# Where a seven-product sum is added to the residual, and which down panels of a gated MLP use seven products

## The chip, the cores and the metric

One core of a Trainium2 chip runs the whole program in one launch. The metric is the device time of an execution in microseconds (us), the median of several runs. Engines are called as in the profile: PE (TensorE, the matmuls), DVE (VectorE), ACT (ScalarE), POOL (GpSimd), SP (SyncE).

## The reference

Two layers of a decoder trunk over 256 tokens of width 2048, in fp32. Layer 0 mixes by gated linear attention, layer 1 by attention with forget gates; both also attend to 256 memory tokens. Behind each mixer stands a gated MLP of hidden width 5632, and this is where the change lies:

```python
def conv_ffn(h, w_up, conv_w, conv_b, w_down):
    u = causal_dwconv(h @ w_up, conv_w, conv_b)
    a, val = split_cols(u, [FFN_HIDDEN, FFN_HIDDEN])
    return (jax.nn.silu(a) * val) @ w_down

        h = rmsnorm(x, norm_ffn[i])
        x = x + conv_ffn(h, ffn_w_up[i], ffn_conv_w[i], ffn_conv_b[i], ffn_w_down[i])
    return rmsnorm(x, norm_final)
```

## The kernel before, in words

**Weights.** They come in units of 512 KB (two chunks of 128 rows by 512 columns and the like, a tile 128x1024) on SP's queue into a ring of slots `raw`. ACT rounds a unit to a high part (`whi`, L259, or L407 in a seven pair), DVE subtracts that for a low part (`wlo`, L260 or L408). The rings have five slots each and, in the MLP, one guest more, named `moremk` (high) and `moremv` (low) in layer 0 and `more` in layer 1. A product of two fp32 matrices is made of three passes of PE: high by high, low activations by high, high by low; each matmul is 128x128 by 128x512 into a bank of PSUM (`acc`, or the work banks `ps_o`, `ps_s`, `ps_t`).

**The residual.** `x[0]` to `x[3]` (x_64 to x_67 in the lists below) lie in SBUF, 512 columns each, two blocks b of 128 tokens. `add_to(f)` (L525) adds a bank or a tile to `x[f][:, b]` on DVE.

**The MLP.** The 44 hidden chunks of 128 are worked in three parts, PARTS = ((0, 16), (16, 28), (28, 44)). An up panel (`up_pair(j)`) makes four hidden chunks, whose results are turned, sent through memory and back (the transfers of L677 and L682, on Pool's queue), run through the convolution (taps, L1445 on ACT, L1452 on DVE) and gated into `m` (names `mix`, A, B). When a part's chunks are ready, its down panels add their products to x: `down_pair(l, p, f, ...)` is a wide panel for x[f] and x[f+1] at once, for f=0 and f=2 in the first two parts and for f=0 in the last. A counter `tick` at each step hands out the convolution's steps.

**Seven products.** `pair_steps` runs such a wide panel unit by unit, each unit one chunk of 128 rows by 1024 columns. For a pair of chunks (k, k+1) listed in `sums`, it uses Winograd's form of the 2x2 block product: seven products p1 to p7 and `x` in place of eight, 21 matmuls in place of 24. It needs sums of activations (made beforehand into `usum` or `dsum` tiles by `token_sums`) and of weights: the low part of w1 (512 columns) and w2, four differences of 512 columns (L464 to L467, in place in `raw`), and the low parts of w3 and w4 (`split_more`, L408). The matmul is at L437. When the last such pair of a panel is done, `early` takes the banks p1, p5, p6, p7 together and adds them to the four tiles of x; the banks of the other four products stay open for the rest of the panel, and `late` adds them to x at the panel's end by `add_to`. `at_step` says at which step which pair is taken, by default a pair at the step of its own number; the single units fill the other steps in order.

Before, part 0 has two pairs: f=0 takes pair 10 by seven products, f=2 pair 4 (FIRST_DOWN = (10,)), and each takes the other by eight. Before the up panels that follow, f=2 of part 0 lets three steps run, then frees the tile `dsum1` for the sums of an up panel (`input_sums(THIRD)`).

A scheduler orders the instructions of each engine, by priority and its own estimates; `issue_after` and `high_priority` steer it.

Of the kernel before, what the change touches and what calls it, by code (L numbers as in the profile page):

```python
# [16 lines left out]
AF = mybir.ActivationFunctionType  # L17
ALU = mybir.AluOpType
# [24 lines left out]
FIRST_DOWN = (10,)  # L43
# [83 lines left out]
def _layout():  # L127

    where, off = {}, 0
    for key, _, kcs, cols, per in _panels():  # L130
        n = sum(c[1] for c in cols)
        units = []
        for u in range(0, len(kcs), per):
            units.append((off, kcs[u : u + per], n))
            off += P * per * n
        where[key] = units
    return where, off
# [17 lines left out]
def _trunk(ctx: ExitStack, tc: tile.TileContext, xt, xtok, memt, wp, wgu, gns, gfin, cnv, par, msk, out):  # L155
    nc = tc.nc
    where, _ = _layout()
    V, S, TE = nc.vector, nc.scalar, nc.tensor
# [4 lines left out]
    x = [rear.tile([P, 2, 512], F32, name=f"x{f}") for f in range(4)]  # L163
# [13 lines left out]
    part = const.tile([P, P], F32, name="part")[:, :C_N]  # L177
# [345 lines left out]
    def add_to(f):  # L523

        return lambda b, a: V.tensor_tensor(x[f][:, b, :], x[f][:, b, :], a, ALU.add)  # L525
# [844 lines left out]
                    steps[f](u)  # L1370


    def down_pair(l, p, f, src, sums, flip, pool, temps, then=None):

        def early(bank):
            t0, t1 = temps()
            S.activation(t0, bank["p1"], AF.Copy)
            add_to(f)(0, t0)
            V.tensor_tensor(t0, bank["p6"], t0, ALU.add)
            V.tensor_tensor(t1, bank["p7"], t0, ALU.add)  # L1380
            add_to(f)(1, t1)
            add_to(f + 1)(1, t1)
            add_to(f + 1)(1, bank["p5"])
            V.tensor_tensor(t0, bank["p5"], t0, ALU.add)
            add_to(f + 1)(0, t0)

        def late(b, h, a):
            held_back = then is not None and h and not b and then.rooms is not None
            with tc.issue_after(then.turned[-1].ins) if held_back else nullcontext():
                add_to(f + h)(b, a)  # L1390
            if then is not None:
                then(f + h, b)

        return pair_steps(where["down", l, p, f], src, sums, flip, pool, early, late, {k: k for k in sums})

    def add_out(key, src, then=None, spare=None, last=None, first=0, hooks=None, late=1):

# [23 lines left out]
    def ffn(l, nx, h, m, more, ys, zs, landing, then, pool, temps, last=None, spare=None):  # L1421
        with tc.tile_pool(name=f"ffn{l}", bufs=1) as fp:
            def held(name, i):
                return pool.tile([P, 2, 4, P], F32R, name=name, tag=f"{name}{i}")
# [12 lines left out]
            count = [0, 0, 0]  # L1437
            sums = {}
# [34 lines left out]
            def input_sums(k):  # L1473

                r = temps(3).rearrange("p (s t) -> p s t", s=2)
                for s in range(2):
                    V.tensor_tensor(r[:, s, :], h[k + s][:, 0, :].bitcast(F32), h[k + s][:, 1, :].bitcast(F32), ALU.add)
                token_sums(r, up_sums[k])
# [28 lines left out]
            def tick(share):  # L1507

                clock[0] += 1
                credit[0] = min(credit[0], 0.0) + share  # L1510
                while returns and returns[0][0] <= clock[0] and not unread[returns[0][1]]:
                    _, slot, back, steps = returns.pop(0)
                    back()
                    unread[slot] = 12
                    waiting.extend(steps)
                while waiting and waiting[0][0] <= clock[0] and credit[0] > 0:
                    _, cost, step = waiting.pop(0)
                    credit[0] -= cost
                    step()
# [34 lines left out]
            def drive(steps, share=1.45):  # L1554
                for k in steps:
                    tick(share if k >= 0 else 0.0)

            def drive_up(j):
                drive(up_pair(j), 1.7 if j // 4 in MORE_IN else 1.45)
# [6 lines left out]
            for p, (lo, hi) in enumerate(PARTS[:-1]):  # L1566
                while done < hi + 4:
                    drive_up(done)
                    done += 4
                src = [m[c % RING] for c in range(lo, hi)]  # L1570
                for f in (0, 2):
                    count[2] += 1
                    steps = down_pair(l, p, f, src, {c - lo: t for c, t in sums.items() if (c in FIRST_DOWN) == (f == 0)}, count[2] % 2, pool,
                                      lambda: (temps(0), temps(1)))
                    if f and not p:
                        for _ in range(3):
                            next(steps)
                            tick(1.45)
                        up_sums[THIRD] = held("dsum", 1)
                        input_sums(THIRD)  # L1580
                    drive(steps)
                sums.clear()
            lo, hi = PARTS[-1]
# [2 lines left out]
                done += 4  # L1586
            p = len(PARTS) - 1
            src = [m[c % RING] for c in range(lo, hi)]
            wide = down_pair(l, p, 0, src, {c - lo: t for c, t in sums.items()}, 0, pool, lambda: (temps(0), temps(1)), then)

            def third(b, a):
                add_to(2)(b, a)
# [37 lines left out]
    def preparing(name, dst, pool, far, kept=None, tag="blk", queue=nc.sync):  # L1630

        n = StreamNorm()
        blocks, rooms, turned_blocks = {}, {}, []
        away, landed = [], []

        def land(z=None):  # L1640

            f, back = away.pop(0)
            if z is None:
                z = pool.tile([P, 4, 4, 2, 32], F32, name="turn", tag="turn", bufs=2) if kept is None else kept[f]
            with tc.issue_after((loads if queue is nc.sync else sent)[-1].ins):
                back(flat(z))
            landed.append((f, z))

        def take():

            f, z = landed.pop(0)
            with tc.issue_after(casts[-1].ins):
                for k in range(4):
                    split_turned(dst, 4 * f + k, z, name)

        def then(f, b):
            n.add(f, b)
            with tc.high_priority(offset=AHEAD):
                if b == 0:
                    blocks[f] = rooms[f]() if f in rooms else pool.tile([P, 4, 4, 2, 32], F32, name="blk", tag=tag, bufs=2)  # L1660
                y = blocks[f]
                turned_blocks.append(V.transpose(y[:, :, :, b, :],
                                                 x[f][:, b, :].rearrange("p (k c i) -> p c k i", c=4, i=32)))
                if b:
                    with tc.issue_after(sent[-1].ins) if queue is nc.gpsimd else nullcontext():
                        away.append((f, far_away(far, flat(y), T, queue)))

        n.rooms = then.rooms = rooms
        then.turned = turned_blocks
        n.land = then.land = land  # L1670
        n.take = then.take = take
        return n, then

    n = gla(nx)
    with tc.tile_pool(name="stash", bufs=1) as st:
        vt = st.tile([P, 2, FOX_H * HD], F32, name="fvt")
        turned3 = vt.rearrange("p b t -> p (b t)").rearrange("p (f q k b j) -> p f q k b j", f=3, q=4, k=4, b=2)
        turned3 = [turned3[:, f] for f in range(3)]

        with tc.tile_pool(name="turn1", bufs=1) as tp:  # L1680
            n2, then = preparing("kv", bufB, tp, dram, turned3, "raw2", nc.gpsimd)
            ys = [const.tile([P, 4, 4, 2, 32], F32, name="yu", tag=tag) for tag in ("mk0", "mv0")]
            fixed = [vt.rearrange("p b t -> p (b t)")[:, 2048 + 512 * i : 2560 + 512 * i] for i in range(2)]

            def temps(i):
                return fixed[i] if i < 2 else tp.tile([P, 512], F32, name="temp", tag=f"temp{i}")

            more = []
            for t, tag in ((mk, "mk1"), (mv, "mv1")):
                parked.append(dram.tile([P, 4 * T], F32, name="park" + tag, tag="park" + tag, bufs=1))  # L1690
                nc.gpsimd.dma_start(parked[-1], t[1].rearrange("p a b -> p (a b)"))
                more.append(const.tile([P, NUNIT], F32R, name="more" + tag, tag=tag))
            ffn(0, n, bufB, bufA, more, ys, turned3, ys, then, tp, temps)
        fox(n2, vt, turned3)
    with tc.tile_pool(name="turn2", bufs=1) as tp:
        n, then = preparing("ffn1", bufA, tp, dram)
# [7 lines left out]
    with tc.tile_pool(name="store", bufs=1) as op:  # L1704
# [16 lines left out]
        def then(f, b):  # L1721
            fin.add(f, b)
            if f == 0 and b == 0:
                S.activation(junk, fin.sums[:, 0, 0:1], AF.Sqrt)
            V.tensor_tensor(x[f][:, b, :], x[f][:, b, :], gf[f], ALU.mult)
# [110 lines left out]
```

## Time and profile before

| what | value |
|---|---|
| median of three runs | 2203.38 us (2202.36 to 2203.61) |
| the profiled execution: its own time | 2202.76 us |
| its span in the profile | 2200.8 us |
| PE busy | 2189.7 us (99%) |
| DVE busy | 1854.8 us (84%) |
| ACT busy | 1441.9 us (66%) |
| POOL busy | 137.2 us (6%) |
| moved by DMA | 515.40 MB, 234 GB/s mean |

The profile is of one execution. Times of instructions count from the start of the span. In rows of the timeline the columns are start, duration, engine, line and operation, tile written <- tiles read, shapes; an "x2" is two instructions run together, and brackets give idle time and who ended it. Instructions are pipelined, so one's duration (1.22 us) is more than the distance of two starts.

### The profile page before, as it was taken

How to read it: one execution, taken by the hardware profiler on the slowest of the kernel's cores; microseconds unless marked ns; L12 is line 12 of the kernel's file. 1: busy time of each engine (PE TensorE's matmuls, PEld its weight loads, DVE VectorE, ACT ScalarE, POOL GpSimd, SP SyncE). 2: the span in 40 equal slices, each digit the busy share in tenths (PEclk: the TensorE clock that was granted, in tenths of full speed). 3: DMA queues.
4: the chain of work that ended last, by engine and by line, in shares of the span. 5: the costliest groups of instructions: out<-in, count | busy, mean ns of one | idle time of the engine just before them, and what ended most of it. 6: DMA issues, size and time to landing. Idle time of an engine off the chain costs nothing.

```text
span 2200.8 us, 30087 instructions
## 1 busy us (share of the span) xinstructions
PE 2189.7 (99%) x10273; PEld 1843.4 (84%) x10273; DVE 1854.8 (84%) x2769; ACT 1441.9 (66%) x2292; POOL 137.2 (6%) x257
## 2 busy tenths in 40 slices
PE   9999999999999999999999999999999999999998
PEld 7888888888888888888888998888888888888886
DVE  7768986679998889899987669768999898988996
ACT  6655655557785668757865555455878567765884
POOL 0000000001110011001010000000110001101100
PEclk9999999999999999999999999999999999999999
DMA  9777566777777577667777766776777657766783
GB/s 365 254 223 225 185 216 218 258 234 259 244 258 243 173 237 257 233 210 241 249 245 238 225 204 226 243 243 235 248 270 245 216 187 262 239 209 231 238 274 107
DMA packets 166289, 515.40 MB, mean 234 GB/s; under 512 B 20780, under 2 KB 42552, under 8 KB 166136
## 3 DMA queue, kind: packets, MB, share of 16 engines
q1 hardware_dynamic: 149064, 460.99, 63.1%
q0 software_dynamic: 16496, 51.71, 7.4%
q8 instruction: 80, 1.31, 0.2%
q10 hardware_dynamic: 576, 0.79, 0.1%
q14 instruction: 73, 0.60, 0.1%
HBM read 469.62 MB, written 43.79 MB: 233 GB/s over the span
## 4 chain that ended last, share of the span: by engine, by line
PE 99%; DMA 0%; DVE 0%; ACT 0%; issue 0%; SPq 0%; DVEq 0%
PE acc L437 30%; PE acc L364 26%; PE ps_s L437 15%; PE ps_o L437 8%; PE ps_t L437 7%; PE acc L290 3%; PE acc L335 3%; PE ps_s L364 2%; PE acc L394 2%; PE acc L288 1%; PE ps_s L1062 0%; DMA raw<-wp 0%; PE ps_o L728 0%; PE ps_s L728 0%; PE ps_s L1335 0%; PE ps_s L1108 0%
## 5 line engine op out<-in xcount | busy, mean ns | idle before, releaser
L260 DVE TENSOR_TENSOR wlo<-raw,whi 128x1024 fp32r<-128x1024 f32 (+2 forms) x608 | 723.7, 1199 | 180.4 <-ACT whi L259 168.6
L259 ACT ACTIVATE whi<-raw 128x1024 fp32r<-128x1024 f32 (+2 forms) x608 | 630.1, 1043 | 368.5 <-PE acc L364 141.5
L364 PE MATMUL acc<-whi,B 128*128 128x512 f32 (+3 forms) x1248 | 290.8, 369 | 0.0
L364 PEld LDWEIGHTS acc<-whi,B 128*128 128x128 f32 x1248 | 226.8, 188 | 28.1
L407 ACT ACTIVATE whi<-raw 128x1024 fp32r<-128x1024 f32 (+1 forms) x166 | 156.4, 942 | 123.2 <-DVE raw L465 39.9
L408 DVE TENSOR_TENSOR wlo<-raw,whi 128x1024 fp32r<-128x1024 f32 (+1 forms) x166 | 178.1, 1076 | 15.6 <-ACT whi L407 9.8
L437 PE MATMUL acc<-whi,B 128*128 128x512 f32 x652 | 172.3, 389 | 0.0
L437 PE MATMUL acc<-whi,mix 128*128 128x512 f32 x636 | 164.9, 389 | 0.0
L364 PE MATMUL acc<-wlo,B 128*128 128x512 f32 (+3 forms) x624 | 159.1, 369 | 0.0
L437 PEld LDWEIGHTS acc<-whi,B 128*128 128x128 f32 x652 | 122.4, 188 | 25.4
L437 PEld LDWEIGHTS acc<-whi,mix 128*128 128x128 f32 x636 | 119.4, 188 | 24.8
L1445 ACT ACTIVATE tap<-fvt,cw 128x256 f32<-128x256 f32 x264 | 123.6, 530 | 9.6 <-DMA fvt<-far 7.9
L1445 ACT ACTIVATE tap<-yzu,cw 128x256 f32<-128x256 f32 x264 | 123.5, 529 | 5.9 <-DMA yzu<-far 4.2
L364 PEld LDWEIGHTS acc<-wlo,B 128*128 128x128 f32 x624 | 114.2, 188 | 14.6
L1452 DVE TENSOR_TENSOR tap<-tap,tap 128x1024 f32<-128x1024 f32 x88 | 106.9, 1215 | 0.1
L437 PE MATMUL ps_s<-whi,mix 128*128 128x512 f32 x350 | 98.5, 389 | 0.0
L437 PE MATMUL acc<-wlo,B 128*128 128x512 f32 x326 | 96.9, 389 | 0.0
L437 PE MATMUL acc<-wlo,mix 128*128 128x512 f32 x318 | 91.7, 389 | 0.0
L437 PE MATMUL ps_s<-whi,B 128*128 128x512 f32 x276 | 78.3, 389 | 0.0
L437 PEld LDWEIGHTS ps_s<-whi,mix 128*128 128x128 f32 x350 | 65.7, 188 | 13.7
L437 PEld LDWEIGHTS acc<-wlo,B 128*128 128x128 f32 x326 | 61.2, 188 | 12.7
L364 PE MATMUL acc<-whi,mix 128*128 128x512 f32 x280 | 70.4, 390 | 0.0
(569 smaller groups left out, 4307.5 us busy)
## 6 DMA issues: line engine op xcount, KB each, us to landing
raw<-wp SPq DMA_DIRECT2D x741, 512.0 KB, 4.6
fvt<-far POOLq DMA_DIRECT2D x100, 128.0 KB, 4.7
raw<-wp SPq DMA_DIRECT2D x32, 384.0 KB, 3.5
far<-yu POOLq DMA_DIRECT2D x22, 512.0 KB, 3.4
far<-yzu POOLq DMA_DIRECT2D x22, 512.0 KB, 3.4
yzu<-far POOLq DMA_DIRECT2D x88, 128.0 KB, 4.5
raw<-wp SPq DMA_DIRECT2D x24, 388.0 KB, 3.8
x<-xtok SPq DMA_DIRECT2D x8, 512.0 KB, 7.3
```

Source lines behind the costliest of these rows:

```text
L259: casts.append(S.activation(hi[:, s], raw[:, s], AF.Copy))
L260: lows.append(V.tensor_tensor(lo[:, s], raw[:, s], hi[:, s].bitcast(F32), ALU.subtract))
L288: mm = TE.matmul(acc[p][c][:, :T], w[:, s], both[:, 0, :], start=False, stop=end and j == 3)
L290: mm = TE.matmul(acc[p][c], w[:, s], both, start=u == j == 0, stop=end and j == 3)
L335: mm = TE.matmul(acc[b][:, :n], src[kcs[j] - base][:, part, b * P : (b + 1) * P], w, start=u == 0 and low == part == j == 0, stop=u == end ...
L364: mm = TE.matmul(acc[b][:, :n], src[kc - base][:, part, b * P : (b + 1) * P], ready[low][:, j * room : j * room + n], start=i == low == pa ...
L394: mm = TE.matmul(acc[b][:, :n], src[kc - base][:, part, b * P : (b + 1) * P], w, start=i == low == part == j == 0, stop=i == end and low = ...
L407: casts.append(S.activation(hi[:, :n], src, AF.Copy))
L408: lows.append(V.tensor_tensor(lo[:, :n], src, hi[:, :n].bitcast(F32), ALU.subtract))
L437: r = TE.matmul(bank[name], x, w, start=name not in begun, stop=last)
L1445: S.activation(by_run(taps[i][:, s, c, i:]), zs[slot][:, :, 2 * c + s], AF.Copy if i else AF.Identity, bias=0.0 if i else w[3], scale=w[2 ...
L1452: V.tensor_tensor(taps[0], taps[0], taps[n][:, :, :, :T], ALU.add)
```

## The change

Two edits. First, `early`: before, DVE added the four sums to x itself (one ACT copy, three additions among the banks, five `add_to`). Now ACT copies p1 to a tile, DVE makes the four sums in four tiles by four additions (L1378 to L1381 of the new kernel), and four transfers on Pool's queue (L1383), 256 KB each, from SBUF to SBUF, add them to x where it lies (`accum_op=ALU.add`). It happens four times in a layer. Second, in part 0 both wide panels take both pairs, 4 and 10, by seven products: f=0 takes pair 4 at step 4 and pair 10 at step 10 of its plan (written {5: 4, 10: 10}, the key being the step), f=2 takes pair 10 at step 5 and pair 4 at step 10. f=2 lets eight steps run before `dsum1` is taken over, with a `tick` share of 0.0 for the steps that `pair_steps` yields as -1.

```diff
@@ -1370,19 +1370,17 @@
                     steps[f](u)
 
 
-    def down_pair(l, p, f, src, sums, flip, pool, temps, then=None):
+    def down_pair(l, p, f, src, sums, flip, pool, temps, then=None, at_step=None):
 
         def early(bank):
-            t0, t1 = temps()
-            S.activation(t0, bank["p1"], AF.Copy)
-            add_to(f)(0, t0)
-            V.tensor_tensor(t0, bank["p6"], t0, ALU.add)
-            V.tensor_tensor(t1, bank["p7"], t0, ALU.add)
-            add_to(f)(1, t1)
-            add_to(f + 1)(1, t1)
-            add_to(f + 1)(1, bank["p5"])
-            V.tensor_tensor(t0, bank["p5"], t0, ALU.add)
-            add_to(f + 1)(0, t0)
+            t = [temps(i) for i in range(4)]
+            S.activation(t[0], bank["p1"], AF.Copy)
+            V.tensor_tensor(t[1], bank["p6"], t[0], ALU.add)
+            V.tensor_tensor(t[2], bank["p7"], t[1], ALU.add)
+            V.tensor_tensor(t[3], bank["p5"], t[2], ALU.add)
+            V.tensor_tensor(t[1], bank["p5"], t[1], ALU.add)
+            for (b, h), part in zip(((0, 0), (0, 1), (1, 0), (1, 1)), t):
+                nc.gpsimd.dma_start(x[f + h][:, b, :], part, accum_op=ALU.add)
 
         def late(b, h, a):
             held_back = then is not None and h and not b and then.rooms is not None
@@ -1391,7 +1389,7 @@
             if then is not None:
                 then(f + h, b)
 
-        return pair_steps(where["down", l, p, f], src, sums, flip, pool, early, late, {k: k for k in sums})
+        return pair_steps(where["down", l, p, f], src, sums, flip, pool, early, late, at_step or {k: k for k in sums})
 
     def add_out(key, src, then=None, spare=None, last=None, first=0, hooks=None, late=1):
 
@@ -1570,12 +1568,11 @@
                 src = [m[c % RING] for c in range(lo, hi)]
                 for f in (0, 2):
                     count[2] += 1
-                    steps = down_pair(l, p, f, src, {c - lo: t for c, t in sums.items() if (c in FIRST_DOWN) == (f == 0)}, count[2] % 2, pool,
-                                      lambda: (temps(0), temps(1)))
+                    steps = down_pair(l, p, f, src, {c - lo: t for c, t in sums.items() if not p or (c in FIRST_DOWN) == (f == 0)}, count[2] % 2, pool,
+                                      temps, at_step=None if p else {5: 10, 10: 4} if f else {5: 4, 10: 10})
                     if f and not p:
-                        for _ in range(3):
-                            next(steps)
-                            tick(1.45)
+                        for _ in range(8):
+                            tick(1.45 if next(steps) >= 0 else 0.0)
                         up_sums[THIRD] = held("dsum", 1)
                         input_sums(THIRD)
                     drive(steps)
@@ -1586,7 +1583,7 @@
                 done += 4
             p = len(PARTS) - 1
             src = [m[c % RING] for c in range(lo, hi)]
-            wide = down_pair(l, p, 0, src, {c - lo: t for c, t in sums.items()}, 0, pool, lambda: (temps(0), temps(1)), then)
+            wide = down_pair(l, p, 0, src, {c - lo: t for c, t in sums.items()}, 0, pool, temps, then)
 
             def third(b, a):
                 add_to(2)(b, a)
```

DVE's order, at the end of panel f=2 of part 0 in layer 0. Before (fvt is one of the temporaries, tap_4117 a tile of the convolution, x_66 and x_67 the halves of this panel's residual):

```order
L525 TENSOR_TENSOR x_67<-x_67,fvt 128x512
L408 TENSOR_TENSOR wlo<-raw,whi 128x512
L1452 TENSOR_TENSOR tap_4117<-tap_4117,tap_4118 128x1024
L464 TENSOR_TENSOR raw<-raw 128x512
L408 TENSOR_TENSOR moremv_4106<-raw,moremk_4103 128x1024
L1452 TENSOR_TENSOR tap_4117<-tap_4117,tap_4119 128x1024
L465 TENSOR_TENSOR raw<-raw 128x512
L466 TENSOR_TENSOR raw<-raw 128x512
L467 TENSOR_TENSOR raw<-raw 128x512
L525 TENSOR_TENSOR x_66<-x_66,acc 128x512
L408 TENSOR_TENSOR wlo<-raw,whi 128x1024
L525 TENSOR_TENSOR x_66<-x_66,acc 128x512
```

The same place in the changed kernel, from the first addition of `early` on (its convolution additions are at L1450):

```order
L1378 TENSOR_TENSOR fvt<-ps_t,fvt 128x512
L408 TENSOR_TENSOR wlo<-raw,whi 128x512
L1379 TENSOR_TENSOR temp<-ps_s,fvt 128x512
L464 TENSOR_TENSOR raw<-raw 128x512
L408 TENSOR_TENSOR wlo<-raw,whi 128x1024
L1380 TENSOR_TENSOR temp<-ps_s,temp 128x512
L1381 TENSOR_TENSOR fvt<-ps_s,fvt 128x512
L465 TENSOR_TENSOR raw<-raw 128x512
L525 TENSOR_TENSOR x_66<-x_66,acc 128x512 x2
L260 TENSOR_TENSOR wlo<-raw,whi 128x1024
L466 TENSOR_TENSOR raw<-raw 128x512
L1450 TENSOR_TENSOR tap_4117<-tap_4117,tap_4118 128x1024
```

and on from there to the low part `moremv` of the up panel's first seven pair:

```order
L525 TENSOR_TENSOR x_67<-x_67,acc 128x512 x2
L467 TENSOR_TENSOR raw<-raw 128x512
L408 TENSOR_TENSOR wlo<-raw,whi 128x1024
L260 TENSOR_TENSOR wlo<-raw,whi 128x1024
L1450 TENSOR_TENSOR tap_4117<-tap_4117,tap_4119 128x1024
L408 TENSOR_TENSOR wlo<-raw_4114,whi 128x1024
L408 TENSOR_TENSOR wlo<-raw,whi 128x512
L408 TENSOR_TENSOR moremv_4106<-raw,moremk_4103 128x1024
```

Before, the last of `early` (the first row) stood ahead of the up panel's weights; now all of `early`, the differences L464 to L467 of the up panel's first pair and the panel's final adds to x_66 and x_67 stand between each other.

PE's order in the up panel that follows, around the end of its first seven pair (B_97 and on are chunks of its input, `dsum` the sums). Before:

```order
L437 MATMUL ps_s<-whi,B_101 128x512 x4
L437 MATMUL ps_t<-whi,B_101 128x512 x2
L437 MATMUL ps_o<-wlo,B_101 128x512
L437 MATMUL ps_s<-wlo,B_101 128x512 x2
L437 MATMUL ps_t<-wlo,B_101 128x512
L437 MATMUL acc<-whi,B_103 128x512 x2
L437 MATMUL acc<-wlo,B_103 128x512
L437 MATMUL ps_o<-moremk_4103,B_104 128x512 x2
L437 MATMUL ps_o<-moremv_4106,B_104 128x512
L437 MATMUL ps_s<-moremk_4103,usum 128x512 x2
L437 MATMUL ps_s<-moremv_4106,usum 128x512
L437 MATMUL ps_o<-whi,B_102 128x512 x2
```

In the changed kernel:

```order
L437 MATMUL acc<-moremv_4106,dsum 128x512
L437 MATMUL ps_s<-moremv_4106,B_100 128x512
L437 MATMUL ps_s<-whi,B_98 128x512 x2
L437 MATMUL ps_s<-wlo,B_98 128x512
L437 MATMUL ps_s<-whi,B_101 128x512 x2
L437 MATMUL ps_s<-wlo,B_101 128x512
L437 MATMUL ps_o<-whi,B_102 128x512 x2
```

Before, all eight matmuls of a unit with the high part ran together (B_101, into three kinds of bank); now the two into the second `ps_s` bank are held back for units B_98 and B_101 and run behind the pair's last low part, shortly ahead of the next unit, B_102.

## The prediction

> **What bounds the kernel now.** First the page: the span, the share of each engine, and the chain that ended last.
>
> ```profile
> span 2200.8 us, 30087 instructions
> PE 2189.7 (99%) x10273; PEld 1843.4 (84%) x10273; DVE 1854.8 (84%) x2769; ACT 1441.9 (66%) x2292; POOL 137.2 (6%) x257
> PE 99%; DMA 0%; DVE 0%; ACT 0%; issue 0%; SPq 0%; DVEq 0%
> ```
>
> TensorE (PE) is busy 2189.7 of 2200.8 us and holds 99% of the chain. The view of its waits names all that it waited for:
>
> ```profile
> PE ps_o L191 <- DVE B L188: 1.5, 1, 1.5
> PE acc L335 <- DVE A L562: 0.3, 1, 0.3
> PE acc L364 <- DVE wlo L260: 0.2, 1, 0.2
> PE acc L394 <- DVE wlo L260: 0.2, 1, 0.2
> ```
>
> That is 2.2 us in all, and none of it stands in a panel that the change touches. The chain in order of time gives the price of one matmul, where 144 of them stand behind each other in 32.64 us:
>
> ```profile
> 881.45 32.64 PE acc L437 x144
> ```
>
> 32.64 / 144 = 0.2267 us. So a matmul that goes is worth 0.2267 us, and work taken from VectorE (DVE) alone is worth nothing, as long as DVE is in time. What the change can lose is therefore read from how late DVE comes where the change puts work. The table of stretches shows DVE over the panel f=2 of part 0 (712.65 to 755.49 us in layer 0) and around it:
>
> ```profile
> 670.00:712.60 42.60, 42.60 (x189) 35.27 (x189) 38.45 (x53) 22.18 (x28) 5.48 (x10) 1.00 0.74 246
> 712.60:755.00 42.40, 42.40 (x188) 35.11 (x188) 36.83 (x44) 28.95 (x43) 0.00 (x0) 1.00 0.48 163
> 755.00:797.00 42.00, 42.00 (x187) 34.75 (x187) 38.57 (x46) 25.26 (x31) 0.00 (x0) 1.00 0.67 237
> ```
>
> Its third column of times is DVE: 38.45 of 42.60, 36.83 of 42.40, 38.57 of 42.00 us. PE has no gap, but DVE has little to spare (4, 5.5 and 3.5 us of some 42). This is the place to look at.
>
> **The matmuls.** A chunk pair by seven products takes 21 matmuls instead of 24. In part 0 f=0 now takes pair 4 as well and f=2 pair 10 as well: two pairs more in each of two layers, 4 × 3 = 12 matmuls fewer, and all lie on the path: 12 × 0.2267 = **-2.72 us**. This is also the most that can be won, but for the 2.2 us of waits elsewhere that the change does not touch.
>
> **DVE's work.** Its durations, from the timeline of DVE, by the distance from one start to the next:
>
> ```profile
> 732.44 2.35 DVE L260 TENSOR_TENSOR wlo<-raw,whi 128x1024 fp32r<-128x1024 f32 x2
> 734.71 1.22 DVE L260 TENSOR_TENSOR moremv<-raw,moremk 128x1024 fp32r<-128x1024 f32 x1
> 735.85 1.22 DVE L1452 TENSOR_TENSOR tap<-tap,tap 128x1024 f32<-128x1024 f32 x1
> 736.98 1.28 DVE L525 TENSOR_TENSOR x<-x,fvt 128x512 f32<-128x512 f32 x2
> 738.18 2.35 DVE L260 TENSOR_TENSOR wlo<-raw,whi 128x1024 fp32r<-128x1024 f32 x2
> ...
> 744.52 0.75 DVE L556 TENSOR_TENSOR mix<-tap,mix 128x256 fp32r<-128x256 f32 x2
> 745.20 0.68 DVE L525 TENSOR_TENSOR x<-x,fvt 128x512 f32<-128x512 f32 x1
> ```
>
> Two 1024-wide low parts take 734.71 - 732.44 = 2.27, one 1.135; two 512-wide additions take 738.18 - 736.98 = 1.20, one 0.60 (0.605 over longer runs). A seven pair costs DVE one low part of 512, three of 1024 and four differences of 512 instead of two low parts of 1024: 0.605 + 3 × 1.135 + 4 × 0.605 - 2 × 1.135 = +4.16; two in a layer, +8.3. Each end of the seven products drops from eight additions to four, 4 × 0.605 = -2.42, four in a layer, -9.7. So DVE gains 1.4 us in a layer, but in part 0 it has 8.3 - 4.8 = 3.5 us more. Off the path, DVE's balance costs nothing; what counts is where the 3.5 us falls.
>
> **The end of panel f=2, part 0.** The panel has lost three matmuls of f=0 ahead of it, and starts where this row stood, at 711.97:
>
> ```profile
> 711.97 0.62 PE L437 MATMUL ps_t<-whi,A 128*128 128x512 f32 x2
> 712.65 1.52 PE L437 MATMUL acc<-whi,mix 128*128 128x512 f32 x6
> 727.38 0.39 PE L437 MATMUL ps_t<-wlo,dsum 128*128 128x512 f32 x1
> 755.49 0.61 PE L437 MATMUL ps_o<-whi,B 128*128 128x512 f32 x2
> ```
>
> Before, the last product p6 was whole at 727.38 + 0.39, 28 us ahead of the next up panel (755.49), and the additions to x were spread over that time. Now pair 4 is the last seven pair, and its p6 low matmul is number 165 of the panel: 711.97 + 164 × 0.2267 = 749.15, whole at 749.54. DVE's in-order queue holds L1378 there, which waits for it; with it 22 instructions stand in DVE's order up to the end of the low part `moremv`, 8 of 1024 and 14 of 512: 8 × 1.135 + 14 × 0.605 = 17.55, so that low part is ready at 767.09. PE asks for it in the first seven pair of the up panel, 80 matmuls behind that p6: 749.15 + 80 × 0.2267 = 767.29. **0.2 us to spare.** The 17.55 us hold no idle time, so each wait put into them beyond 0.2 us comes out at PE.
>
> The accumulating transfers put one there. The residual adds of L525 at the panel's end (x_66, then x_67) must wait for the transfers into the same bytes to land. The x_66 transfer from `temp` is issued when L1379 is done, 749.54 + 3 × 0.605 = 751.36; DVE reaches the second add to x_66 after eight instructions of 512 and one of 1024, 8 × 0.605 + 1.135 behind 749.54, at 755.52. Cover: 4.16 us. (For x_67: 4.69.) So with a landing time L a layer loses max(0, L - 4.16 - 0.20) us. No transfer in the trace adds to its target. The nearest rows, all issued by Pool:
>
> ```profile
> far<-yu POOLq DMA_DIRECT2D x22, 512.0 KB, 3.4
> fvt<-far POOLq DMA_DIRECT2D x100, 128.0 KB, 4.7
> L682 POOL DMA_DIRECT2D fvt<-far x100: 550/552/583, 506.7 to 1152.5; - x100
> DMA to landing us min/median/max: 2.7/4.6/9.3
> DMA to landing us min/median/max: 2.9/3.4/9.4
> out<-x SPq DMA_DIRECT2D x4, 256.0 KB, 3.4
> ```
>
> The two lines of landing are those of L682 (into SBUF) and of L677 (out of SBUF). So L lies between 2.7 and 9.4; I take 4.4, between the medians and nearer to the transfers that land in SBUF as these do: 0.04 us. At 2.7 it costs nothing, at 9.4 it costs 5.0 us a layer.
>
> By the Trainium skill ("DMA: Bandwidth & Descriptors", section "Anatomy of one DMA — SWDGE (gpsimd) path") such a transfer takes about 2.0 us and its bytes at 436 GB/s, an estimate of 2.6 us for 256 KB; that would leave this term at zero. The trace's 128 KB into SBUF, with 4.7 us, are slower than it says.
>
> Two smaller terms stand in the same up panel. In PE's new order the products of unit 1 wait for the fourth low part, so between the last reading of one high part (B_98) and the first use of the one that takes its slot (B_102) stand 4 matmuls, 0.91 us, and the split takes one ACT operation:
>
> ```profile
> L259 ACT ACTIVATE whi<-raw 128x1024 fp32r<-128x1024 f32 (+2 forms) x608 | 630.1, 1043 | 368.5 <-PE acc L364 141.5
> ```
>
> 1.04 - 0.91 and the hand-overs give some 0.2 us. And the second seven pair's `w3` low part ends 6 × 1.135 + 9 × 0.605 = 12.3, with two short splits (L556, 745.20 - 744.52 = 0.68 for two) 12.9 us, behind unit 5's low part, where PE asks for it 55 matmuls = 12.47 us behind it: 0.3 us with the hand-over. Bounds of both: nothing, if the slot comes free in other places first, and twice as much. The sum for the place is 0.5 us a layer, and layer 1 has the same order row for row: **+1.1 us**.
>
> **Elsewhere.** The ends of f=0 in part 0, of f=2 in part 1 and of the wide last panel have the same four transfers, but 7 us or more lie between them and the adds that wait, and DVE has 2.4 us less to do in the last two: nothing, as long as L stays below 7; above it they too would hold DVE. Pool issues 16 transfers more in a layer, 0.55 us each as in the row of L682; Pool is busy 137.2 us, and what stands behind them on its queue belongs to an up panel's return more than 20 us later: nothing. SP's weight loads keep their order; the added 8 MB of traffic from SBUF to SBUF is 2% of the page's bytes: nothing at 0.48 of DMA share.
>
> **Sum.** -2.72 + 1.1 = -1.6 us. Made against the profiled execution's 2202.76: 2201.1. The median of the three runs is 2203.38, 0.62 above it: **2201.7**.
>
> **The rivals.** *All of it is won.* DVE is a little quicker than my sum over the 22 instructions and L is under 4.3: 2203.38 - 2.72 = 2200.7. For it: PE shows no gap today at places where DVE is 92% busy; against: 0.2 us to spare is less than my rows agree to.
>
> *The transfers land late.* An adding transfer has to read its target as well as its source. If it then takes twice as long as the plain one of 256 KB (3.4), L = 6.8, and each layer loses 6.8 - 4.36 = 2.44: -2.72 + 4.88 + 1.0 = +3.2, 2206.6. It is even at L = 5.2 and slower by over 0.2% from L = 7.4; at the 9.3 that L682's slowest took, +8.2, 2211.6. For it: the longest rows; against: the medians, and DMA is busy 0.48 of this stretch. The Trainium skill ("Collectives: The Full Stack", section "The bandwidth ceiling: the fold count and why AG ≠ RS ≠ AR") says that a reducing step takes two source reads and runs at half the rate of a copy; by it the sum would be this rival's. No run here shows such a transfer yet.
>
> *No change at all*, that the extra products are eaten by DVE's 3.5 us: they would have to be lost whole at the panel's end, 1.75 us a layer at L near 5.2. It lies between the forecast and the second rival.
>
> **How the numbers follow.** Forecast (2201.7, stalls of 0.2 to 1 us a layer) 47%; all won (2200.7) 29%; late landings 20%, of which 12% end below +4.4 us and 8% above; something that gains more 2%, something else that costs more 2%. A measurement tells 0.2%, 4.4 us, from no change. Faster by more would need more than the 12 matmuls: 0.02; slower by more: 0.08 + 0.02 = 0.10; within: 0.88. The range goes from all won less the 0.6 us by which profile and median differ, 2200.1, to a landing of 6.3 us, -2.72 + 3.88 + 1.0 = +2.1, 2205.5. What lies above (late landings beyond that) and below is some 16%.
>
> **What would show it.** Right: PE 10261 instructions, busy some 2.7 us less; its waits a few tenths at the first up panel behind part 0 (near 766 to 775 us, and 1033 us later in layer 1), for `moremv` or `wlo` of L408 or `whi` of L259; the transfers of L1383 land in 4 to 5 us. Wrong: a wait of DVE's L525 for the transfers of more than a microsecond, then PE waits of the same size; PE waits at other panels; or a landing time under 3 us with the stall still there.

## The result and the profile after

The changed kernel takes **2206.20 us** (median of 15 runs, 2204.12 to 2211.42), the one before 2202.77 (median of 15, 2201.92 to 2203.61): a ratio of 1.0017, interval 1.0010 to 1.0024, some 3.4 us slower. The forecast was 2201.7, its range ended at 2205.5. Against the full saving of the 12 matmuls, 2202.77 - 2.72 = 2200.05, the changed kernel has lost 6.1 us. The profiled execution took 2211.42 us, the slowest of the 15: against the same full saving it has lost 11.4 us, so the stalls read below are larger than those of the median run.

The page of the changed kernel, with its span, the share of the engines and the row of 24 of its 32 new transfers (the other eight carry `x<-fvt`):

```profile
span 2209.6 us, 30107 instructions
PE 2191.3 (99%) x10261; PEld 1841.6 (83%) x10261; DVE 1852.0 (84%) x2761; ACT 1445.8 (65%) x2300; POOL 165.1 (7%) x289
x<-temp POOLq DMA_DIRECT2D x24, 256.0 KB, 6.4
```

PE has its 12 matmuls fewer (10273 to 10261) and is still busy 1.6 us longer. DVE fell by 2.8 us, which is the 1.4 us a layer of the prediction. Pool is busy 27.9 us more for the 32 transfers. The view of waits names what PE waits for:

```profile
PE ps_o L437 <- ACT whi L259: 2.6, 4, 1.9
PE acc L437 <- ACT whi L259: 1.6, 1, 1.6
PE ps_o L191 <- DVE B L188: 1.5, 1, 1.5
PE ps_s L1334 <- ACT p L738: 1.4, 1, 1.4
PE ps_o L437 <- DVE wlo L260: 0.7, 1, 0.7
PE ps_s L437 <- ACT whi L407: 0.7, 1, 0.7
PE acc L364 <- ACT whi L259: 0.3, 1, 0.3
```

All rows but L191's are new, and nearly all name a weight split of ACT or DVE. (L1334's lies in the attention of layer 1, which the change leaves alone; experiments without transfers show it too, with 0.5 to 1.0.) The places of the loss are read from the starts of the matmuls, which lie apart by more than their 0.2267 us. In layer 0 that is so at 769 us (0.5 us in all), at 822 to 830 (4.8) and at 870 to 873 (some 1.7). In layer 1, 1033 us later, it is so at the same three places: 1807 to 1810 (0.7), 1863 to 1865 (0.4) and 1908 (2.2). The first of the three is the place that the prediction spoke of; the others lie one and two up panels later.

The table of stretches covers the last panel of part 0 and the three up panels behind it, first in the changed kernel, then in the one before, whose row of 755 to 797 us the prediction has shown:

```profile
711.00:755.00 44.00, 44.00 (x195) 36.44 (x195) 36.17 (x49) 26.76 (x41) 3.23 (x4) 1.00 0.63 198
755.00:797.00 42.00, 41.77 (x184) 34.13 (x183) 39.92 (x47) 25.99 (x31) 0.24 (x1) 1.00 0.70 233
797.00:840.00 43.00, 40.60 (x170) 32.57 (x169) 34.08 (x40) 29.27 (x45) 5.49 (x10) 0.96 0.68 218
840.00:882.00 42.00, 41.00 (x179) 33.14 (x178) 38.52 (x51) 29.94 (x49) 5.48 (x10) 1.00 0.70 245
```

```profile
711.00:755.00 44.00, 44.00 (x196) 36.44 (x195) 38.42 (x47) 28.95 (x43) 0.00 (x0) 1.00 0.49 167
797.00:840.00 43.00, 43.00 (x191) 35.63 (x190) 37.55 (x47) 33.05 (x51) 5.54 (x10) 1.00 0.72 233
840.00:882.00 42.00, 42.00 (x187) 34.75 (x187) 41.72 (x52) 35.20 (x58) 5.50 (x10) 1.00 0.75 245
```

Read the third column of times, DVE. In the panel it is given one seven pair more and four additions less, 4.16 - 2.42 = some 1.7 us more by the prediction's prices, and yet it does 36.17 us instead of 38.42: it stands idle for 7.8 us, where it was for 5.6. The view of its waits says in this stretch for what:

```profile
DVE x L525 <- DMA x<-temp: 3.1, 2, 1.6
DVE wlo L260 <- ACT whi L259: 2.6, 3, 1.2
DVE fvt L1378 <- PE ps_t L437: 2.1, 1, 2.1
DVE x L525 <- DMA x<-fvt: 0.2, 1, 0.2
```

It waits 3.3 us for landings at f=0's end and 2.1 us for p6 of the late pair; the 2.6 us for ACT's splits were 2.5 before. What DVE didn't do there comes behind, in panels with little room: the last row of before has 41.72 of 42.00 us. And the third row of the changed kernel holds only 170 matmuls, at a mean granted clock of 0.96.

How lateness of DVE comes to PE can be followed in layer 0 over three engines. First come DVE's transposes that end the first up panel, from its timeline, before and after:

```profile
797.32 0.70 DVE L1492 STREAM_TRANSPOSE yu<-fvt 128x512 f32<-128x512 f32 x1
798.57 0.70 DVE L1492 STREAM_TRANSPOSE yu<-temp 128x512 f32<-128x512 f32 x1
```

```profile
798.78 0.70 DVE L1490 STREAM_TRANSPOSE yu<-fvt 128x512 f32<-128x512 f32 x1
801.77 0.70 DVE L1490 STREAM_TRANSPOSE yu<-temp 128x512 f32<-128x512 f32 x1
```

The second is 3.2 us later, though PE had come 1.4 us earlier to f=2's end and lost 0.5 since. Pool, which waits for it, sends the panel's first half away at 799.56 before and at 802.84 after. Its rows go on to the second half and to the loads that bring both back:

```profile
799.56 0.56 POOL L677 DMA_DIRECT2D far<-yu  x1 [109.12 <-DVE yu L1492]
802.54 0.56 POOL L677 DMA_DIRECT2D far<-yu  x1 [2.42 <-DMA far<-yu]
803.10 0.57 POOL L682 DMA_DIRECT2D fvt<-far  x1
```

```profile
802.84 0.56 POOL L677 DMA_DIRECT2D far<-yu  x1 [47.60 <-DVE yu L1490]
805.23 0.55 POOL L677 DMA_DIRECT2D far<-yu  x1 [1.83 <-DVE yu L1490]
808.37 4.38 POOL L682 DMA_DIRECT2D fvt<-far  x8 [2.59 <-DMA far<-yu]
```

The loads go out 5.3 us later. ACT stands at the first convolution tap until they have landed, and the weight splits that follow in its order start only behind it (before, then after):

```profile
812.78 2.91 ACT L1445 ACTIVATE tap<-fvt,cw 128x256 f32<-128x256 f32 x7 [2.64 <-DMA fvt<-far]
```

```profile
819.11 2.12 ACT L1443 ACTIVATE tap<-fvt,cw 128x256 f32<-128x256 f32 x5 [8.44 <-DMA fvt<-far]
```

ACT is idle for 8.44 us where it was for 2.64, and PE then waits for its splits. PE's timeline of the changed kernel shows this, and behind the waits a few slow matmuls:

```profile
821.13 0.39 PE L437 MATMUL acc<-moremv,usum 128*128 128x512 f32 x1
822.22 1.19 PE L437 MATMUL ps_s<-whi,usum 128*128 128x512 f32 x4 [0.69 <-ACT whi L407]
823.48 0.73 PE L437 MATMUL ps_s<-wlo,usum 128*128 128x512 f32 x2
825.84 2.93 PE L437 MATMUL acc<-whi,B 128*128 128x512 f32 x6 [1.63 <-ACT whi L259]
828.57 1.18 PE L437 MATMUL acc<-wlo,B 128*128 128x512 f32 x3
829.59 0.62 PE L437 MATMUL ps_t<-whi,usum 128*128 128x512 f32 x2
830.04 1.98 PE L437 MATMUL acc<-whi,B 128*128 128x512 f32 x8
```

From 825.84 to 828.57 six matmuls start, one per 0.455 us, twice the 0.2267. The granted clock of this stretch, the third number from the end, is 0.51:

```profile
825.80:828.60 2.80, 2.76 (x7) 2.18 (x8) 2.78 (x3) 2.80 (x4) 0.00 (x0) 0.51 0.24 64
```

From 821.13 to 830.04 there are 18 matmuls, 4.1 us of work in 8.9: 4.8 lost, of it some 1.7 to the slow matmuls. This is the one such place: in no other kernel's trace does a stretch of 20 us between 400 and 2180 us have a granted clock under 1.00.

In layer 1 the same chain costs less. ACT stands 5.54 us at the tap there, and PE loses only 0.4 us at 1863. The largest loss of layer 1, at 1908, has another wait ahead of it, that of a split for its weights:

```profile
1857.00 2.12 ACT L1443 ACTIVATE tap<-yzu,cw 128x256 f32<-128x256 f32 x5 [5.54 <-DMA yzu<-far]
1905.31 1.06 ACT L259 ACTIVATE whi<-raw 128x1024 fp32r<-128x1024 f32 x1 [1.51 <-DMA raw<-wp]
```

That load was issued at 1897.38, after 1.4 us of waiting for a low part of DVE (L408), and took 7.9 us to land, against a median of 4.5. Whether DVE's lateness is behind this wait too was not tried; the return is in any case not the only place where PE's time goes.

### The profile page after: what moved, and what is told of

The parts are those of the page before. It is cut to its first block, busy times and chain, and to the rows that moved or that the text cites. A ratio compares the mean times of both kernels' runs of the same rounds, so it can differ in the third digit from the quotient of the medians.

```text
span 2209.6 us, 30107 instructions
## 1 busy us (share of the span) xinstructions
PE 2191.3 (99%) x10261; PEld 1841.6 (83%) x10261; DVE 1852.0 (84%) x2761; ACT 1445.8 (65%) x2300; POOL 165.1 (7%) x289
## 4 chain that ended last, share of the span: by engine, by line
PE 93%; issue 4%; DMA 1%; ACT 1%; DVE 1%; POOL 0%; SPq 0%; DVEq 0%; ACTq 0%; POOLq 0%
PE acc L437 27%; PE acc L364 26%; PE ps_s L437 14%; PE ps_o L437 7%; PE ps_t L437 6%; PE acc L335 3%; PE acc L290 2%; PE ps_s L364 2%; PE acc L394 2%; PE acc L288 1%; PE ps_s L1062 0%; DMA fvt<-far 0%; ACT whi L259 0%; PE ps_o L728 0%; DMA far<-y 0%
## 5 line engine op out<-in xcount | busy, mean ns | idle before, releaser
L260 DVE TENSOR_TENSOR wlo<-raw,whi 128x1024 fp32r<-128x1024 f32 (+2 forms) x601 | 715.7, 1200 | 196.8 <-ACT whi L259 185.1
L259 ACT ACTIVATE whi<-raw 128x1024 fp32r<-128x1024 f32 (+2 forms) x601 | 622.8, 1043 | 370.7 <-PE acc L364 140.3
L364 PEld LDWEIGHTS acc<-whi,B 128*128 128x128 f32 x1248 | 226.8, 188 | 28.1
L407 ACT ACTIVATE whi<-raw 128x1024 fp32r<-128x1024 f32 (+1 forms) x180 | 169.5, 946 | 95.8 <-DVE raw L465 32.7
L408 DVE TENSOR_TENSOR wlo<-raw,whi 128x1024 fp32r<-128x1024 f32 (+1 forms) x180 | 194.0, 1082 | 22.3 <-ACT whi L407 17.4
L437 PE MATMUL acc<-whi,mix 128*128 128x512 f32 x644 | 168.7, 389 | 0.1
L437 PE MATMUL acc<-whi,B 128*128 128x512 f32 x606 | 163.1, 392 | 1.6 <-ACT whi L259 1.6
L437 PEld LDWEIGHTS acc<-whi,B 128*128 128x128 f32 x606 | 114.4, 189 | 25.9 <-ACT whi L259 2.1
L1450 DVE TENSOR_TENSOR tap<-tap,tap 128x1024 f32<-128x1024 f32 x88 | 106.9, 1215 | 1.7 <-ACT tap L1443 1.7
L437 PE MATMUL ps_s<-whi,mix 128*128 128x512 f32 x314 | 90.2, 389 | 0.0
L437 PE MATMUL ps_s<-whi,B 128*128 128x512 f32 x296 | 85.5, 389 | 0.0
L437 PEld LDWEIGHTS acc<-wlo,mix 128*128 128x128 f32 x322 | 60.4, 188 | 12.6
```

The costliest lines, as they stand in the source:

```text
L259: casts.append(S.activation(hi[:, s], raw[:, s], AF.Copy))
L260: lows.append(V.tensor_tensor(lo[:, s], raw[:, s], hi[:, s].bitcast(F32), ALU.subtract))
L364: mm = TE.matmul(acc[b][:, :n], src[kc - base][:, part, b * P : (b + 1) * P], ready[low][:, j * room : j * room + n], start=i == low == pa ...
L407: casts.append(S.activation(hi[:, :n], src, AF.Copy))
L408: lows.append(V.tensor_tensor(lo[:, :n], src, hi[:, :n].bitcast(F32), ALU.subtract))
L437: r = TE.matmul(bank[name], x, w, start=name not in begun, stop=last)
```

## The experiments

There were two theories at first. **A:** the extra seven pair in the last panel of part 0 makes DVE late, and PE is reached by the way just read. **B:** the accumulating transfers, which land in 6.4 us in the median and take Pool 0.87 us each, are the cost. The medians of the kernel before beside the runs were 2202.9 to 2203.0 us. "Lost" below is a kernel's distance from that (for the changed kernel from 2202.77), plus the 0.2267 us for each matmul that it saves.

| kernel | median, us | ratio to before (interval) | matmuls fewer | lost, us |
|---|---|---|---|---|
| changed kernel | 2206.20 | 1.0017 (1.0010 to 1.0024) | 12 | 6.1 |
| transfers only | 2203.14 | 1.0002 (0.9993 to 1.0011) | 0 | 0.2 |
| pairs only | 2211.59 | 1.0037 (1.0025 to 1.0050) | 12 | 11.3 |
| transfers, pair in f=0 only | 2201.70 | 0.9997 (0.9988 to 1.0006) | 6 | 0.1 |
| transfers, pair in f=2 only | 2209.72 | 1.0030 (1.0019 to 1.0042) | 6 | 8.1 |
| changed, taps later | 2203.57 | 1.0003 (0.9994 to 1.0012) | 12 | 3.3 |
| changed, pairs of f=2 at 3 and 7 | 2199.92 | 0.9987 (0.9978 to 0.9996) | 12 | -0.4 |
| pairs in f=0 of parts 0 and 1 | 2205.78 | 1.0012 (1.0003 to 1.0021) | 12 | 5.5 |
| before, DVE work added | 2205.69 | 1.0012 (1.0003 to 1.0021) | 0 | 2.7 |
| pairs at 3 and 7, no transfers | 2202.87 | 0.9999 (0.9990 to 1.0008) | 12 | 2.7 |
| changed, pairs of f=2 at 4 and 8 | 2199.60 | 0.9987 (0.9978 to 0.9996) | 12 | -0.6 |
| changed, pairs of f=2 at 2 and 5 | 2200.69 | 0.9990 (0.9982 to 0.9999) | 12 | 0.5 |

The intervals reach some 1.5 to 3 us to either side, so a "lost" below 2 us can't be told from none.

**The two halves alone.** First comes the changed kernel with the choice of pairs of before; `dsum1` is taken over after three steps again:

```diff
-  steps = down_pair(l, p, f, src, {c - lo: t for c, t in sums.items() if not p or (c in FIRST_DOWN) == (f == 0)}, count[2] % 2, pool,
-                    temps, at_step=None if p else {5: 10, 10: 4} if f else {5: 4, 10: 10})
+  steps = down_pair(l, p, f, src, {c - lo: t for c, t in sums.items() if (c in FIRST_DOWN) == (f == 0)}, count[2] % 2, pool, temps)
...
-  for _ in range(8):
+  for _ in range(3):
...
```

> The accumulating transfers alone, with the seven pairs of the kernel before (no matmul fewer). The changed kernel came out 3.4 us above the one before, 6.1 above what 12 matmuls fewer should give. Theory A, late DVE: the extra seven pair in the last panel of part 0 makes DVE late, the next up panel's transposes, return and taps come late, ACT waits with the weight splits behind it, PE starves. Then this kernel, whose DVE has less to do, is level with the one before: 2202.8, within 0.7. Theory B, the transfers themselves: they land late (median 6.7 us), hold DVE's adds and Pool's queue, and load the DMA engines. Then it is 4 to 6 us slower than before, 2207 to 2209.

It took 2203.14 us, level with before. Theory B falls as the whole cause; and the 9.7 us a layer that DVE is spared bring nothing either. The other half is the new choice of pairs with the additions of before in `early`:

```diff
-            t = [temps(i) for i in range(4)]
...
-                nc.gpsimd.dma_start(x[f + h][:, b, :], part, accum_op=ALU.add)
+            t0, t1 = temps(0), temps(1)
+            S.activation(t0, bank["p1"], AF.Copy)
+            add_to(f)(0, t0)
...
+            add_to(f + 1)(0, t0)
```

> The four extra seven pairs alone, with the additions of the kernel before on DVE (12 matmuls fewer, 2.7 us). Theory A: DVE has 4 additions more at each end of a seven product than in the changed kernel, so it is at least as late behind the last panel of part 0: the loss of some 6 us stays or grows, 2206 to 2211. Theory B: no transfers, no loss: 2200.1, within 0.7.

It took 2211.59 us, 11.3 us lost and a little above A's range: the pairs alone are worse than the whole change. The transfers are worth 5.4 us where the pairs are. But the way is another here. PE waits already in the first up panel, for `moremv` among others, which is the wait that the prediction had priced:

```profile
PE acc L437 <- ACT whi L407: 1.6, 2, 0.8
...
PE acc L437 <- DVE more L408: 1.3, 2, 1.0
PE acc L437 <- DVE moremv L408: 1.2, 2, 1.0
```

In layer 0 the matmuls lose 4.9 us between 760 and 800 us and none at the two later places. So this run bears out that late DVE costs time, but not the way over the return.

**Which panel.** These kernels have the transfers and the extra pair in one of the panels, first f=0, then f=2 (the conditions alone are shown; the other panel keeps its steps of before, and with f=0's pair `dsum1` is taken over after three steps):

```diff
-  if not p or (c in FIRST_DOWN) == (f == 0)
+  if (not p and not f) or (c in FIRST_DOWN) == (f == 0)
```

> The transfers, and the extra seven pair in f=0 of part 0 alone (6 matmuls fewer, 1.36 us); f=2 as before. Theory A: f=0 has the whole of f=2 behind it for DVE to catch up: the saving without the loss, 2201.4, within 0.7. Theory B: the loss stays: 2206 to 2208.

```diff
-  if not p or (c in FIRST_DOWN) == (f == 0)
+  if (not p and f) or (c in FIRST_DOWN) == (f == 0)
```

> The transfers, and the extra seven pair in f=2 of part 0 alone (6 matmuls fewer, 1.36 us); f=0 as before. Theory A: the last pair of f=2 is late as in the changed kernel and the loss of some 6 us with it: 2206 to 2208. Theory B: the loss stays as well: 2206 to 2208; so this run and the third tell the theories apart together.

They took 2201.70 and 2209.72 us. f=0's pair loses nothing that can be told; f=2's pair loses all, even 2 us more than both together and more than either theory had (2206 to 2208). In its trace DVE waits 5.7 us in this panel for a tile that a transfer of f=0's end still reads, which would fit the 2 us; it was not tried:

```profile
DVE temp L1475 <- DMA x<-temp: 5.7, 1, 5.7
```

**What hands the lateness on.** The taps of that up panel are put off, so that four more weight splits stand ahead of the first tap in ACT's order:

```diff
-PUT_OFF = {16: 21}
+PUT_OFF = {16: 21, 20: 14}
```

> The changed kernel, with the convolution taps of the up panel behind part 0 due 14 steps after its end instead of 7 or 8 (so four more weight splits stand ahead of the first tap in ACT's order); nothing else changed, 12 matmuls fewer as there. Theory A1: what costs is ACT, which stands at its first tap for the late return (8.4 us in the profile of the changed kernel) with the splits behind it. Then most of the loss goes: 2200.5 to 2203. Theory A2: DVE itself is 3.5 us late through three up panels that leave it no time, and the tap is only one of the places where that shows: PE then waits elsewhere for low parts and slots, 2204.5 to 2207.

2203.57 lies between the two ranges: 2.6 us of the 6.1 come back in the median, though the runs of the two kernels overlap (2201.40 to 2206.36 against 2204.12 to 2211.42). PE's waits at 822 to 830 and at 870 are gone, but others stand in a later up panel, at 960 to 964 us and 1033 us behind it in layer 1:

```profile
PE ps_s L437 <- ACT whi L407: 1.6, 2, 0.8
...
PE ps_o L437 <- ACT whi L259: 0.5, 2, 0.2
PE ps_t L437 <- ACT whi L407: 0.4, 2, 0.2
```

So the tap's wait is one way to PE (A1), and DVE's lateness (or that of the taps moved with it) finds another (A2). The two are not told apart further.

**Place or amount.** The same pairs stand earlier in f=2, and `dsum1` is taken over earlier with them (parts of the changed lines):

```diff
-  {5: 10, 10: 4} if f
+  {3: 10, 7: 4} if f
...
-  for _ in range(8):
+  for _ in range(6):
```

> The changed kernel, with the two seven pairs of f=2 in part 0 at steps 3 and 7 instead of 5 and 10 (and the sums for the up panel made after 6 steps instead of 8). Same work for every engine. Theory A1/A2 with the place deciding: the last sums are whole some 15 us before the panel's end, DVE gets its work done in the panel where it has 5 us idle, all of the saving comes: 2200.3, within 1.0. Rival A3, the amount decides: DVE's 3.5 us more in part 0 come out wherever the pairs stand: 2204 to 2207.

2199.92 us is all of the saving, with the same work. Two more kernels have the pairs at steps 4 and 8 (and 7 for the 8 of the loop), then at 2 and 5 (and 5):

> The changed kernel with the pairs of f=2 in part 0 at steps 4 and 8 (5 and 10 gave 2206.2, 3 and 7 gave 2199.9). The last p6 is whole two steps, 5.4 us, earlier than in the changed kernel. Theory A2: the loss goes with the time that DVE stands idle ahead of the last p6 (7.8 us idle in the panel at 5 and 10, 3.5 at 3 and 7): 2200.5 to 2203. If only a late end of the sums hurts, as a threshold at the panel's end: 2200, as at 3 and 7.

> The changed kernel with the pairs of f=2 in part 0 at steps 2 and 5, earlier again. Theory A2: nothing more to win, as PE has no wait left at 3 and 7, but DVE's work of two pairs may now collide with the end of f=0 and its landings: 2199.9 to 2202.

They took 2199.60 and 2200.69 us. So it is no slope, as had been expected for 4 and 8: between pairs at 4 and 8 and pairs at 5 and 10 the loss appears whole. Whether the first pair, the second or the earlier takeover of `dsum1` decides was not separated. The three kernels that lose nothing have these rows in the panel's stretch (3 and 7, then 4 and 8, then 2 and 5):

```profile
711.00:755.00 44.00, 44.00 (x195) 36.45 (x195) 40.48 (x53) 31.22 (x48) 3.46 (x4) 1.00 0.77 225
```

```profile
711.00:755.00 44.00, 44.00 (x196) 36.41 (x195) 39.47 (x53) 30.98 (x46) 3.47 (x4) 1.00 0.71 216
```

```profile
711.00:755.00 44.00, 44.00 (x196) 36.42 (x195) 39.86 (x52) 32.67 (x50) 3.47 (x4) 1.00 0.78 226
```

DVE does 3.3 to 4.3 us more in the panel than in the changed kernel (36.17), and that is the work that was carried on there. With 4 and 8 the chain is early again: the panel's first half goes away at 797.95, its four loads follow from 801.14, and ACT takes 11 taps in a row from 808.18 with no wait ahead of them.

```profile
808.18 4.77 ACT L1443 ACTIVATE tap<-fvt,cw 128x256 f32<-128x256 f32 x11
```

One more thing differs in these kernels. With 3 and 7 and with 4 and 8 Pool's order puts the loads of the first half ahead of the second half's send, where the changed kernel sends both halves first. With 2 and 5 both halves are sent first, as before and in the changed kernel, and nothing is lost either: the sends stand at 800.16 and 803.08, the first load at 803.83 instead of 808.37. So the other order on Pool is not needed for the saving.

**Early pairs without transfers.** The pairs stand at 3 and 7, with the additions of before on DVE:

> The two seven pairs of f=2 at steps 3 and 7, which gave 2199.9 with the transfers, now with the additions of the kernel before on DVE and no transfer (12 matmuls fewer). With late pairs the same exchange cost 5.4 us (2211.6 against 2206.2). DVE gets 4 x 0.605 = 2.4 us more at each of the two ends of part 0's panels, 4.8 in all; with early pairs it stood idle for 3.5 us in the last panel (44.00 - 40.48). Theory A2: what does not fit, some 1.3 us in a layer, is carried on and shows in part: 2200.5 to 2203.5. If the place of the pairs alone decides, 2200.3, within 0.7, and the transfers are worth nothing here; if the amount alone decides, 2205 or more.

It took 2202.87 us, 2.7 us lost, as A2 had it. So both matter: the place (2211.59 to 2202.87 without transfers) and the amount that DVE has to do (2202.87 to 2199.92 by the transfers).

**Lateness alone.** The kernel before is given work for DVE at the end of f=2 of part 0, in its `late`:

```diff
+            if p == 0 and f == 2 and h == b == 0:
+                idle, _ = temps()
+                with tc.high_priority(offset=2 * AHEAD):
+                    for _ in range(7):
+                        V.tensor_tensor(idle, x[f][:, b, :], a, ALU.add)
```

> The kernel before, no transfer and no pair more, but with seven additions of 512 columns (7 x 0.605 = 4.2 us of DVE) into a tile that nobody reads, which can't run before the first bank of the last panel of part 0 is whole and stand in DVE's order over the next 20 us. Theory A: DVE late behind this panel is enough to lose time: 2206 to 2212. Rival: the loss needs the new order of PE, the transfers or the later early sums: 2203, within 1.0.

It took 2205.69 us, 2.7 us slower, a little under A's range: 4.2 us of work for DVE, which ran from 752.9 to 771.7 us, are enough, with no pair and no transfer more. PE then waits in the next up panel for low and high parts, and loses 1.3 us at 780 and 1.2 at 1815; at the later places it loses nothing. So lateness of DVE is enough to cost time, and again not by the return.

**A rule that fell.** This kernel has one more pair in f=0 of part 1, with another down panel behind it, and f=2 of part 0 as before (the condition alone is shown):

```diff
-  if (not p and not f) or (c in FIRST_DOWN) == (f == 0)
+  if not f or c not in FIRST_DOWN
```

> The transfers, the extra seven pair in f=0 of part 0 (2201.7 by itself), and an extra seven pair in f=0 of part 1 as well, chunk 20, which only f=2 took so far; f=2 of both parts as in the kernel before. 12 matmuls fewer than before in all. Theory A: a pair in a panel that has another down panel behind it costs nothing: 2200.3, within 0.7. If a pair's 4.2 us of DVE work are paid anywhere: 2202 to 2204.

It took 2205.78 us, 5.5 us lost, more than either alternative had. The largest wait is not in part 1's panels, but behind the MLP, where layer 1 begins (1114 us), for ACT's splits:

```profile
PE acc L364 <- ACT whi L259: 2.8, 1, 2.8
```

"A down panel behind it" is thus no measure of what a pair costs. By which chain it reaches that far was not tried.

## Why the prediction was wrong

**What held.** PE bounds the kernel, and a matmul less is worth 0.2267 us: the kernels that lose nothing come out at -0.6 to +0.5 us from it. The balance of DVE was right (-2.8 us). The place was right as the origin of the loss: the last seven pair of f=2 in part 0. At the panel's end p6 was whole at 748.89 (749.54 forecast), and the low part `moremv` ready at 765.24 + 1.22 = 766.46 (767.09), by DVE's timeline:

```profile
748.89 0.69 DVE L1378 TENSOR_TENSOR fvt<-ps_t,fvt 128x512 f32<-128x512 f32 x1 [2.11 <-PE ps_t L437]
...
765.24 1.22 DVE L408 TENSOR_TENSOR moremv<-raw,moremk 128x1024 fp32r<-128x1024 f32 x1
```

The stall for the ring's slot there, some 0.2 us forecast, measured 0.4 to 0.5 (769 us); the 0.3 us for the second pair's low part did not show.

**The landing.** The estimate of 4.4 us fits the place. The four transfers at the end of f=2 in layer 0 landed so, and no add waited for them:

```profile
DMA to landing us min/median/max: 3.3/3.8/6.8
```

Over all 32 the median was 6.7 us (3.2 to 10.4), as the second rival had it, and at f=0's end, where the prediction put the cover at 7 us, four took 7.3 to 10.1 and held DVE's adds for 3.3 us. PE did not wait there: the transfers with f=0's pair lose 0.1 us. What the 3.3 us add where f=2's pair is late as well was not separated, but without any transfer the loss is larger (11.3). So that rival had the landing time and the sign, and it came near the time by luck (2206.6 against 2206.20): its place and mechanism were not those at work. The Trainium skill ("Collectives: The Full Stack", section "The bandwidth ceiling: the fold count and why AG ≠ RS ≠ AR") puts the half rate of a reducing step in a ring collective down to two source reads. The ratio of 6.4 us to the plain transfer's 3.4 is near that, but the 3.8 us at f=2's end is not, so no run here shows that the second read is the cause. The 2.6 us that the prediction estimated from the Trainium skill ("DMA: Bandwidth & Descriptors", section "Anatomy of one DMA — SWDGE (gpsimd) path") lay under every landing measured (3.2 at the least).

**The step that failed** is the sum for "the end of panel f=2" together with "elsewhere". It asked whether DVE comes in time for one low part, found 0.2 us, and let the lateness end there. But 0.2 us was what was left of DVE's lead at one place. Behind that place DVE stayed late, since the next panels have only 3.5, 5.5 and 0.3 us to spare (38.57 of 42.00, 37.55 of 43.00, 41.72 of 42.00 before). In the changed kernel the work that came too late was not the low part but the up panel's return: transposes, two passes through Pool's queue, then a tap ahead of the splits in ACT's order. The prediction said of Pool that "what stands behind them on its queue belongs to an up panel's return more than 20 us later: nothing". That was right of Pool's time and wrong of the return. The row of 840 to 882 us was not looked at. A loss of 0.5 us a layer was forecast; 6.1 us were lost in the two layers in the median. In the profiled execution some 7 us of the loss lie in layer 0 and some 3 in layer 1, and 1.7 of those in layer 0 fall to matmuls at about half their rate.

That lateness of DVE at this place suffices to cost time is shown (work alone: 2.7 us), and that the late place of f=2's pairs makes the loss is shown (2199.60 against 2206.20). By which way the lateness reaches PE is only in part shown. Putting the taps off brought back 2.6 of the 6.1 us, so the return is one way in the changed kernel; the rest is read from the trace only. The runs with pairs only and with DVE work only lose their time in the first up panel instead, without the return.

The lowest median is that of the changed kernel with f=2's pairs at steps 4 and 8: 2199.60 us, 3.3 us under before, with an interval that excludes no change (0.9978 to 0.9996). Steps 3 and 7 can't be told from it (2199.92).

## What to carry to other kernels

Where an engine that takes its work in order is busy for some 90% of a stretch, as DVE was here, lateness that it takes on in one panel need not end at the next reader. Add up its idle time panel by panel until the debt is paid, and check every chain that starts from it in that time. Sums that can only be taken late belong early enough that their work fits where the engine has idle time: moving two pairs by one and two steps was worth 6.6 us here, more than twice the 2.7 us of matmuls that they were to save.

## What was not expected of the hardware

A transfer of 256 KB from SBUF to SBUF that adds took 6.4 us to land in the median of 24 (3.2 to 10.4 over all 32). The nearest plain transfer of that size, `out<-x` on SP's queue, took 3.4. The landing was slow where DMA was busy: 7.3 to 10.1 us at f=0's end, where the DMA share was 0.98 (698 to 718 us), and 3.3 to 6.8 at f=2's end, where it was 0.76 (742 to 760 us). The 24 held Pool for 0.87 us in the median to issue, against 0.55 for a plain load.

After waits of 0.69 and 1.63 us, PE ran six matmuls at half its rate (0.455 us each) at a granted clock of 0.51, so there the waits cost more than themselves. A single wait of 1.88 us at 1908 was not followed by this: the granted clock from 1908.2 to 1911 us was 1.00. What tells the two apart was not tried.

Runs of the changed kernel spread over 7.3 us (2204.12 to 2211.42), those of before over 1.7. A return whose transfers land now sooner, now later would fit that, but it was not tried.
